# Splitting a gated chunk one chunk later in the feed-forward block of a decoder layer

## The chip, the cores and the metric

The kernel runs on one core of a Trainium2 chip. The metric is the device time of one execution in microseconds, as a median over runs. The profile is one more execution, with its own time; its clock starts at the first instruction of the span. The engines are named as in the profile: PE multiplies matrices and PEld loads their stationary operand, DVE and ACT do element work, POOL does a little of it, and SP issues nearly all DMA transfers in the order in which they stand in its queue.

## The reference

The reference is one decoder layer over 256 tokens of width 1024 in float32: a mixer of causal pooling and block attention, cross-attention into 256 memory tokens, and a dense gated feed-forward network of width 2816, each followed by a residual sum and a layer norm. The part that the change touches is the feed-forward network:

```python
def swiglu(h, w_gate, w_up, w_down):
    return (jax.nn.silu(h @ w_gate) * (h @ w_up)) @ w_down

        h = layer_norm(DEEPNORM_ALPHA * h + swiglu(h, w_gate[l], w_up[l], w_down[l]),
                       ln3_g[l], ln3_b[l])
```

## The kernel before

All large products are made of three matmuls. Each float32 operand is split into a high part, which is the operand rounded by a cast, and a low part, which is the operand minus its high part; the product is high by high, high by low and low by high (`three`, lines 256 to 258). A weight is loaded raw by a DMA from SP's queue (line 80), cast on ACT into its high part (line 99) and subtracted on DVE into its low part (line 100). The weights come as one long stream of pieces w0 to w124, each 128 partitions by 1024 numbers, 512 KB. Seven raw buffers and eight pairs of high and low buffers rotate: the cast of piece i writes the buffers of piece i - 8, and the load of piece i writes the raw buffer of piece i - 7. A piece is prepared (cast, subtracted, and further loads issued) while the matmuls of earlier pieces are being recorded, so casts, subtractions and loads stand in the engines' queues between other work, at the place where the program asked for them.

The feed-forward network works in 11 chunks of 256 columns of the hidden width, numbered 0 to 10. Chunk c uses pieces w(59+4c) to w(62+4c), which hold 256 columns of `w_gate` beside 256 of `w_up`. Per chunk there are eight steps of the inner dimension, each with three matmuls for either of two token tiles, so 48 matmuls with 512 output columns; the two results stand in two of four rotating PSUM banks, `pg`. Then, for either token tile, ACT takes the silu of the gate half (`gated`, line 784) and DVE multiplies it by the other half (line 785) into `sg`. This frees the bank. Four banks are two chunks' worth: PE may work on chunk c + 1 while chunk c waits for `gated`, and no further.

The product with `w_down` needs the gated values with the hidden dimension on the partitions, so each chunk is turned round through DRAM, in three recorded steps. `gated_out` transposes 32 by 32 blocks on DVE into `gs` (line 340) and writes them to DRAM as `gd` (line 343). `gated_in` reads them back as `gr` in four DMAs (line 350); these wait for the write. `gated_split` splits what came back into the high and low parts `gTh` (ACT, line 319) and `gTl` (DVE, line 320). `gs` and `gr` share three rotating buffers.

The order of each engine's queue is the order of the program text, which is written out by hand. The matmuls of a chunk are a generator; `run(gu, n)` records n more of its eight steps, and the three turning steps of the chunk before stand between them. `gated(c)` is recorded when the chunk's matmuls are.

After chunk 10 the generator `dn` records the product with `w_down`, pieces w103 to w124, one row of 128 hidden numbers each. Its first 16 rows go into four accumulators at once, which take the same four PSUM banks as `pg`: a row is six matmuls for token tile 0, into the banks that chunk 9 used, and then six for token tile 1, into the banks of chunk 10. Each half row is one step of `run(dn, n)`. The last six rows, w119 to w124, are done accumulator by accumulator, with the last layer norm behind each. Rows 2c and 2c + 1 use the values of chunk c.

Of the kernel before, what the change touches and what calls it, by code (L numbers as in the profile page):

```python
# [24 lines left out]
NFC = DFF // CW  # L25
# [16 lines left out]
class Stream:  # L42
# [61 lines left out]
    def get(self, numbers, k):  # L104

        n = self.src[numbers[0]].shape[1]
        self.prepare(numbers[k // n] + 1)
        self.asked += 1
        if not self.held and self.asked % self.pace == 0:
            self.prepare(min(self.used + AHEAD, len(self.tiles) + 1))  # L110
        hi, lo = self.tiles[numbers[k // n]]
        return hi[:, k % n, :], lo[:, k % n, :]
# [13 lines left out]
def decoder_layer(  # L126
# [18 lines left out]
    def bank(name):  # L145
        return pb.tile([P, 512], F32, tag="b", name=name)

    def accbank(name):
        return pa.tile([P, 512], F32, tag="acc", name=name)
# [130 lines left out]
    def proj_n(pss, numbers, yT, last=True):  # L280

        for k in range(KD):
            for t, ps in pss.items():
                three(ps, pair(yT, ALL, k, slice(t * P, (t + 1) * P)), ws.get(numbers, k), k == 0, k == KD - 1)
            if last:
                ws.done(numbers, k)
            yield

    def proj_rows(acc, chunks, get, pieces, first, last, free, again=False):

        last_k = sum(ws.rows(numbers) for numbers in chunks) - 1
        k0 = 0
        for numbers in chunks:
            nk = ws.rows(numbers)
            for t in sorted({piece[0] for piece in pieces}):
                for j in range(nk):
                    k = k0 + j
                    y = pair(get(k), ALL, slice(t * P, (t + 1) * P))
                    hi, lo = ws.get(numbers, j)
                    for piece in pieces:  # L300
                        if piece[0] == t:
                            s = slice(*piece[1:])
                            three(acc[piece], y, (hi[:, s], lo[:, s]), first and k == 0, last and k == last_k,
                                  again)
                    if free and t == pieces[-1][0]:
                        ws.done(numbers, j)
                    yield
            k0 += nk

    def run(gen, n=None):  # L310

        while n is None or n > 0:
            if next(gen, gen) is gen:
                return False
            n = None if n is None else n - 1
        return True

    def split(h, l, ps):
        nc.scalar.copy(h, ps)  # L319
        nc.vector.tensor_sub(l, ps, r32(h))  # L320
# [14 lines left out]
    def turned(blocks, n, name):  # L335

        st = sp.tile([P, 4, n, 32], F32, name=f"{name}s", tag="pair", bufs=3)
        for at, src in blocks:
            m = src.shape[1]
            nc.vector.transpose(st[:, :, at:at + m, :].rearrange("p j m b -> p m j b"),  # L340
                                src.rearrange("p m (j b) -> p m j b", b=32))
        via = hp.tile([P, 4, n * 32], F32, name=f"{name}d", tag="hop")
        nc.sync.dma_start(via, st.rearrange("p j m b -> p j (m b)"))
        return via

    def landed(via, n, name):

        raw = sp.tile([P, 4, n, 32], F32, name=f"{name}r", tag="pair", bufs=3)
        for j in range(4):
            nc.sync.dma_start(raw[32 * j:32 * (j + 1)].rearrange("p i m b -> p i (m b)"),  # L350
                              via[:, j, :].rearrange("(i a) r -> a i r", i=4))
        return raw
# [235 lines left out]
    class Norm:  # L588
# [11 lines left out]
        def sum(self, c0, c1, acc):  # L600
            s = slice(c0, c1)
            nc.vector.scalar_tensor_tensor(self.r[:, s], self.tok[:, s], ALPHA, acc, op0=OP.mult, op1=OP.add)  # L602
# [34 lines left out]
    def project(chunks, get, held, pieces=PIECES):  # L637

        acc = {piece: accbank("acc") for piece in PIECES}
        if pieces != PIECES:
            (*_, (_, _, c), _), last = pieces, PIECES[-1]
            acc[pieces[-2]], acc[pieces[-1]] = acc[last][:, :c - last[1]], bank("acc")[:, :last[2] - c]
        head, rest = chunks[:-held], chunks[-held:]
        done = sum(ws.rows(numbers) for numbers in head)
        if head:
            yield from proj_rows(acc, head, get, PIECES, True, pieces != PIECES, True)
        ws.prepare(ws.used + AHEAD)
        ws.prepare(ws.used + W_BUFS, nc.gpsimd)  # L650
        ws.held = True
        for piece in pieces:
            yield from proj_rows(acc, rest, lambda k: get(done + k), [piece], not head or piece[1] % 512 != 0, True,
                                 piece == pieces[-1], bool(head) and pieces != PIECES)
            yield piece, acc[last] if pieces != PIECES and piece == pieces[-2] else acc[piece]
# [125 lines left out]
    def gated(c, t, ps):  # L781

        sg = sgs[c][:, :, t, :]
        nc.scalar.activation(sg, ps[:, :CW].rearrange("p (f b) -> p f b", f=2), AF.Silu, bias=0.0, scale=1.0)  # L784
        nc.vector.tensor_mul(sg, sg, ps[:, CW:].rearrange("p (f b) -> p f b", f=2))  # L785
# [3 lines left out]
    def gated_out(c):  # L789
        via[c] = turned([(0, sgs[c].rearrange("p f t b -> p (f t) b"))], 4, "g")  # L790

    def gated_in(c):
        via[c] = landed(via[c], 4, "g")

    def gated_split(c):
        i, f = divmod(2 * c, KD)
        h, l = [g[:, f:f + 2, :].rearrange("p f (t i b) -> p (f t) i b", t=T, i=4) for g in gT[i]]
        split(h, l, via[c].rearrange("p i m b -> p m i b"))
# [12 lines left out]
    for c in range(1, NFC):  # L811
        sgs.append(sp.tile([P, 2, T, P], F32, name="sg", tag="pr", bufs=PR_BUFS))
        pss = {t: accbank("pg") for t in range(T)}
        gu = proj_n(pss, c_gu[c], h2T)
        run(gu, 1)
        gated_out(c - 1)
        run(gu, 2)
        gated_in(c - 1)
        run(gu, 4)
        gated_split(c - 1)  # L820
        run(gu)
        for t in range(T):
            gated(c, t, pss[t])
# [4 lines left out]

    pieces = PIECES[:3] + ((1, 512, 768), (1, 768, D))
    dn = project(c_dn, lambda k: (gT[k // KD][0][:, k % KD], gT[k // KD][1][:, k % KD]), 6, pieces)  # L830
    run(dn, 4)
    gated_out(NFC - 1)
    run(dn, 8)
    gated_in(NFC - 1)
    run(dn, 12)
    gated_split(NFC - 1)
    def finish(norm, t, at=None):

# [82 lines left out]
```

## Time and profile before

| | |
|---|---|
| median of 3 runs | 397.5 us (397.42 to 398.53) |
| the profiled execution's own time | 396.49 us |
| its span, first to last instruction | 394.7 us |
| mean granted TensorE clock | 0.978 |
| PE busy, share of the span | 374.2 us, 95% |
| DVE busy | 253.2 us, 64% |
| ACT busy | 175.2 us, 44% |
| DMA moved | 77.69 MB, mean 197 GB/s |

The rows of the profile's page name an engine, a line of the kernel, the tile written and the tile read, and how often. "Idle before it" is the time in which the engine stood still just before such an instruction, and the arrow names what came last of those things that it had to wait for. A row of a timeline gives the start in the span, the duration, and the same names. Matmuls are pipelined: the row of one lasts 0.39 us, but the next starts 0.23 us after it, so the starts are what counts.

### The profile page before, as it was taken

Reading aid. Unit: us, or ns where it says so; the run is one execution under the profiler, and the core shown is the slowest. Engines: PE = TensorE matmul, PEld = TensorE weight load, DVE = VectorE, ACT = ScalarE, POOL = GpSimd, SP = SyncE. Lnnn points to the kernel's source line nnn. Section 1 sums busy time; section 2 is a strip of 40 time slices with the busy share of each in tenths; the row PEclk is TensorE's granted clock in tenths of the full one; section 3 lists DMA queues with packets and bytes.
Section 4 is the critical chain, followed back from the end, with each engine's and each line's share of the span. In section 5 each row is a group of like instructions: output and inputs, shape, how many; then the busy total and the mean of one; then the engine's idle time right before and its main releaser. Section 6 shows DMA issues by size and latency. Waiting matters only on the chain.

```text
span 394.7 us, 5499 instructions
## 1 busy us (share of the span) xinstructions
PE 374.2 (95%) x2076; PEld 323.2 (82%) x2076; DVE 253.2 (64%) x371; ACT 175.2 (44%) x263; POOL 19.4 (5%) x31
## 2 busy tenths in 40 slices
PE   9999999999999999999999999999999719999991
PEld 9997989998888999988788888888787607888881
DVE  5768889754897765756895654556665355435175
ACT  5656677544244645543183553333555233344000
POOL 1000038000010000001000000000000000000000
PEclk9999999999999999999999999999999957999998
DMA  8996766658239644232058666765778765640011
GB/s 253 413 413 228 249 232 200 208 183 289 83 112 387 259 149 160 81 134 108 0 161 346 226 215 225 263 216 203 248 229 269 277 217 182 215 132 0 2 50 57
DMA packets 29386, 77.69 MB, mean 197 GB/s; under 512 B 3376, under 2 KB 10160, under 8 KB 29232
## 3 DMA queue, kind: packets, MB, share of 16 engines
q1 hardware_dynamic: 28784, 76.95, 55.6%
q10 hardware_dynamic: 576, 0.39, 0.3%
q8 instruction: 16, 0.26, 0.3%
q14 instruction: 10, 0.08, 0.1%
HBM read 73.40 MB, written 3.93 MB: 196 GB/s over the span
## 4 chain that ended last, share of the span: by engine, by line
PE 64%; DMA 16%; DVE 7%; ACT 5%; SPq 3%; issue 3%; ACTq 0%; DVEq 0%
DMA gd<-gs 11%; PE acc L256 9%; PE acc L257 9%; PE acc L258 9%; PE pqk L391 6%; PE pxq L274 6%; PE pxk L274 6%; DMA gr<-gd 5%; PE pu L274 3%; SPq L350 3%; PE xv L258 2%; PE xv L256 2%; PE xv L257 2%; DVE gs L340 2%; ACT sg L784 1%
## 5 line engine op out<-in xcount | busy, mean ns | idle before, releaser
L320 DVE TENSOR_TENSOR gTl<-gr,gTh 128x512 fp32r<-128x512 f32 x11 | 7.6, 692 | 50.9 <-ACT gTh L319 50.9
L319 ACT CAST gTh<-gr 128x512 fp32r<-128x512 f32 x11 | 6.8, 620 | 67.4 <-DMA gr<-gd 67.4
L613 POOL TENSOR_TENSOR rs<-rs,mhalf 128x1 f32<-128x1 f32 x6 | 5.4, 893 | 313.8 <-DVE rs L612 313.8
L256 PE MATMUL acc<-w103h,gTh 128*128 128x512 f32 x4 | 2.3, 578 | 11.2 <-DVE sg L785 11.2
L602 DVE SCALAR_TENSOR_TENSOR r<-h,acc 128x256 f32<-128x256 f32 (+1 forms) x10 | 5.1, 520 | 10.9 <-PE acc L258 10.9
L256 PEld LDWEIGHTS acc<-w103h,gTh 128*128 128x128 f32 x4 | 1.0, 248 | 12.5 <-DVE sg L785 12.4
L428 ACT ACTIVATE pr<-pr,mx 128x128 f32<-128x128 f32 (+1 forms) x16 | 7.1, 445 | 6.8 <-DVE mx L459 6.8
L605 DVE BATCH_NORM_STATS2 st<-r 128x6 f32<-128x512 f32 (+1 forms) x14 | 8.1, 580 | 0.5
L319 ACT CAST h2Th<-tp 128x512 fp32r<-128x512 f32 x4 | 2.3, 587 | 13.5 <-PE tp L330 13.4
L785 DVE TENSOR_TENSOR sg<-sg,pg 128x256 f32<-128x256 f32 x22 | 8.3, 414 | 0.0
L428 ACT ACTIVATE xpr<-xs,mx 128x256 f32<-128x256 f32 x8 | 3.7, 468 | 10.2 <-DVE mx L439 10.2
L618 DVE SCALAR_TENSOR_TENSOR r<-r,mv,g 128x512 f32<-128x512 f32 x11 | 7.8, 745 | 0.0
L340 DVE STREAM_TRANSPOSE gs<-sg 128x512 f32<-128x512 f32 x11 | 7.7, 704 | 0.0
L784 ACT ACTIVATE sg<-pg 128x256 f32<-128x256 f32 x22 | 7.3, 377 | 0.1
L503 POOL TENSOR_TENSOR win<-win 128x269 f32<-128x269 f32 (+2 forms) x6 | 6.5, 1082 | 0.5
L503 POOL TENSOR_TENSOR win<-upad 128x271 f32<-128x271 f32 x4 | 3.5, 872 | 54.3 <-ACT upad L531 54.3
L433 DVE RECIPROCAL sm<-sm 128x2 f32<-128x2 f32 x12 | 2.0, 167 | 5.9 <-ACT xpr L428 4.5
L624 DVE SCALAR_TENSOR_TENSOR h<-r,rs,b 128x512 f32<-128x512 f32 x8 | 5.6, 747 | 0.0
L319 ACT CAST h1Th<-tp 128x512 fp32r<-128x512 f32 x4 | 2.3, 587 | 7.1 <-PE tp L330 7.1
L330 PEld LDWEIGHTS tp<-ident,h 128*128 128x128 f32 x32 | 3.9, 141 | 1.6 <-issue 0.7
L330 PE MATMUL tp<-ident,h 128*128 128x128 f32 x32 | 4.8, 273 | 0.3 <-DVE h L624 0.3
L362 PE MATMUL busy<-const-float32-0.0 128*128 128x128 f32 x18 | 4.2, 428 | 0.8 <-PEq L885 0.8
(1091 smaller groups left out, 1422.8 us busy)
## 6 DMA issues: line engine op xcount, KB each, us to landing
gd<-gs SPq DMA_DIRECT2D x11, 256.0 KB, 3.7
gr<-gd SPq DMA_DIRECT2D x44, 64.0 KB, 2.1
g<-in_ln_g SPq DMA_DIRECT2D x3, 512.0 KB, 5.1
b<-in_ln_b SPq DMA_DIRECT2D x3, 512.0 KB, 7.5
wr<-in_w_qkv SPq DMA_DIRECT2D x5, 256.0 KB, 4.7
mr<-in_mem_t SPq DMA_DIRECT2D x1, 1024.0 KB, 11.7
xt<-in_x SPq DMA_DIRECT2D x1, 1024.0 KB, 8.3
xr<-in_x_t SPq DMA_DIRECT2D x3, 256.0 KB, 6.3
```

Source lines behind the costliest of these rows:

```text
L256: nc.tensor.matmul(ps, wa, ya, start=start, stop=False, skip_group_check=part)
L257: nc.tensor.matmul(ps, wa, yb, start=False, stop=False, skip_group_check=part)
L258: nc.tensor.matmul(ps, wb, ya, start=False, stop=stop, skip_group_check=part)
L274: nc.tensor.matmul(pss[f], w[:, s], y, start=k == 0 and f == 0 and n == 0, stop=k == KD - 1 and n == 2, skip_group_check=True)
L319: nc.scalar.copy(h, ps)
L330: nc.tensor.transpose(ps[:, k * P:(k + 1) * P], tok[:, (k0 + k) * P:(k0 + k + 1) * P], ident)
L340: nc.vector.transpose(st[:, :, at:at + m, :].rearrange("p j m b -> p m j b"), src.rearrange("p m (j b) -> p m j b", b=32))
L350: nc.sync.dma_start(raw[32 * j:32 * (j + 1)].rearrange("p i m b -> p i (m b)"), via[:, j, :].rearrange("(i a) r -> a i r", i=4))
L391: nc.tensor.matmul(qk[i][:, f, :], w[:, c * P:(c + 1) * P], y, start=k == 0 and f == 0 and w is hi and y is x_hi, stop=k == KD - 1 and w i ...
L428: nc.scalar.activation(dst[:, j, :], src[:, j, :], AF.Exp, bias=mx[:, j:j + 1], scale=sign, accum_out=sm[:, j:j + 1])
L503: nc.gpsimd.tensor_add(nxt[:, 2 * n - 1:], cur[:, 2 * n - 1:], cur[:, n - 1:PADW + S - n])
L784: nc.scalar.activation(sg, ps[:, :CW].rearrange("p (f b) -> p f b", f=2), AF.Silu, bias=0.0, scale=1.0)
```

## The change

The step `gated_split` moves from chunk c + 1, where it stood behind the seventh of eight matmul steps, to chunk c + 2, behind the third. The step `gated_in` stays in chunk c + 1 and moves from behind the third matmul step to behind the fifth. Behind the last chunk, in the product with `w_down`, the splits of chunks 9 and 10 both have to follow; the three steps of chunk 10 move forward there. No instruction is added or removed.

```diff
@@ -815,9 +815,10 @@
         run(gu, 1)
         gated_out(c - 1)
         run(gu, 2)
+        if c > 1:
+            gated_split(c - 2)
+        run(gu, 2)
         gated_in(c - 1)
-        run(gu, 4)
-        gated_split(c - 1)
         run(gu)
         for t in range(T):
             gated(c, t, pss[t])
@@ -828,11 +829,13 @@
 
     pieces = PIECES[:3] + ((1, 512, 768), (1, 768, D))
     dn = project(c_dn, lambda k: (gT[k // KD][0][:, k % KD], gT[k // KD][1][:, k % KD]), 6, pieces)
+    run(dn, 2)
+    gated_out(NFC - 1)
+    run(dn, 2)
+    gated_split(NFC - 2)
     run(dn, 4)
-    gated_out(NFC - 1)
-    run(dn, 8)
     gated_in(NFC - 1)
-    run(dn, 12)
+    run(dn, 10)
     gated_split(NFC - 1)
```

In ACT's queue, at the end of the last chunks, `gTh` is the high part of a chunk read back, `sg` the silu of a chunk's two token tiles, and `w106h` and the like are casts of weights:

```order
 L784 ACTIVATE sg<-pg 128x2x128 x2
 L99 CAST w106h<-w106r 128x1024
 L99 CAST w107h<-w107r 128x1024
+L319 CAST gTh_2047<-gr 128x512
 L99 CAST w108h<-w108r 128x1024
 L99 CAST w109h<-w109r 128x1024
-L319 CAST gTh_2047<-gr 128x512
 L784 ACTIVATE sg<-pg 128x2x128 x2
 L99 CAST w110h<-w110r 128x1024
 L99 CAST w111h<-w111r 128x1024
+L319 CAST gTh_2047<-gr 128x512
```

Here the first silu pair is chunk 9's and the second chunk 10's. The split that stood directly ahead of chunk 10's silu, that of chunk 9, now stands behind it and behind two casts; between the two silu pairs there is now the split of chunk 8, between the second and the third cast. DVE's queue is changed in the same way, with the subtractions and the multiplications of `sg` in place of casts and silus.

In SP's queue, in a chunk of the middle, with the write of a turned chunk (line 343), its four reads (line 350) and loads of weights (line 80):

```order
 L343 DMA gd<-gs 128x512
 L80 DMA w82r<-in_w_gu 128x1024
+L80 DMA w83r<-in_w_gu 128x1024
 L350 DMA gr<-gd 32x4x128 x4
-L80 DMA w83r<-in_w_gu 128x1024
 L80 DMA w84r<-in_w_gu 128x1024
```

The four reads now stand behind one more load of weights than before.

## The prediction

> **What bounds the kernel now.** I read the page first, to see which engine is the limit, then the list of waits.
>
> ```profile
> PE 374.2 (95%) x2076; PEld 323.2 (82%) x2076; DVE 253.2 (64%) x371; ACT 175.2 (44%) x263; POOL 19.4 (5%) x31
> L256 PE MATMUL acc<-w103h,gTh 128*128 128x512 f32 x4 | 2.3, 578 | 11.2 <-DVE sg L785 11.2
> ```
>
> ```profile
> PE acc L256 <- DVE sg L785: 11.2, 2, 9.1
> PE pg L256 <- DVE sg L785: 0.2, 1, 0.2
> ACT gTh L319 <- DMA gr<-gd: 67.4, 10, 8.3
> ```
>
> PE works 95% of the span, so most of what happens on other engines costs nothing. But PE has one large wait, 11.2 us in two pieces, at w103, the first row of the product with `w_down`. What it waits for there is DVE's multiplication of `sg`, which frees a PSUM bank. So the question is why a chunk's `sg` is late. The third wait row is the suspect: ACT stands 67.4 us in ten waits, before casting `gTh`, for data read back from DRAM. PE's timeline shows what this costs.
>
> ```profile
> 213.84 0.39 PE L256 MATMUL pg<-w67h,h2Th 128*128 128x512 f32 x1
> ...
> 301.06 0.39 PE L258 MATMUL pg<-w98h,h2Tl 128*128 128x512 f32 x1
> 301.65 0.50 PE L256 MATMUL pg<-w99h,h2Th 128*128 128x512 f32 x1 [0.20 <-DVE sg L785]
> ...
> 309.03 0.39 PE L258 MATMUL pg<-w101h,h2Tl 128*128 128x512 f32 x1
> ...
> 312.43 0.39 PE L258 MATMUL pg<-w102h,h2Tl 128*128 128x512 f32 x1
> 314.89 0.50 PE L256 MATMUL acc<-w103h,gTh 128*128 128x512 f32 x1 [2.08 <-DVE sg L785]
> ...
> 315.93 0.59 PE L257 MATMUL acc<-w103l,gTh 128*128 128x512 f32 x1
> 316.31 0.63 PE L258 MATMUL acc<-w103h,gTl 128*128 128x512 f32 x1
> 326.08 0.79 PE L256 MATMUL acc<-w103h,gTh 128*128 128x512 f32 x1 [9.14 <-DVE sg L785]
> ...
> 329.64 0.40 PE L258 MATMUL acc<-w104h,gTl 128*128 128x512 f32 x1
> ...
> 331.97 0.39 PE L256 MATMUL acc<-w105h,gTh 128*128 128x512 f32 x1
> ```
>
> The undisturbed step from matmul to matmul is (312.43 - 309.03) / 15 = 0.227 us, so a chunk of 48 takes 10.88 us. Chunk 2 begins at 213.84 (w67), chunk 10 at 301.65 (w99) and ends at 312.43 + 0.23 = 312.66. ACT's rows for the same stretch:
>
> ```profile
> 211.32 1.06 ACT L99 CAST w73h<-w73r 128x1024 fp32r<-128x1024 f32 x1 [1.25 <-PE pg L258]
> 219.72 0.62 ACT L319 CAST gTh<-gr 128x512 fp32r<-128x512 f32 x1 [7.34 <-DMA gr<-gd]
> 220.25 0.65 ACT L784 ACTIVATE sg<-pg 128x256 f32<-128x256 f32 x2
> ...
> 300.44 0.66 ACT L784 ACTIVATE sg<-pg 128x256 f32<-128x256 f32 x2
> ...
> 313.69 0.65 ACT L784 ACTIVATE sg<-pg 128x256 f32<-128x256 f32 x2
> ...
> 317.06 1.05 ACT L99 CAST w109h<-w109r 128x1024 fp32r<-128x1024 f32 x1
> 324.35 0.62 ACT L319 CAST gTh<-gr 128x512 fp32r<-128x512 f32 x1 [6.24 <-DMA gr<-gd]
> 324.87 0.65 ACT L784 ACTIVATE sg<-pg 128x256 f32<-128x256 f32 x2
> ```
>
> ACT takes its queue in order, and each split stands directly ahead of the next chunk's silu. So the silu of chunk 1, whose matmuls were done when chunk 2 began, runs 220.25 - 213.84 = 6.4 us late, and that of chunk 10 runs 324.87 - 312.66 = 12.2 us late. The silus follow a ring: silu, transposition, write to DRAM, read, split, next silu. Its last two rounds took 313.69 - 300.44 = 13.25 us and 324.87 - 313.69 = 11.18 us, both longer than PE's 10.88. The chain of waits shows which part made the longer one long, the write:
>
> ```profile
> 303.93 5.76 DMA gd<-gs
> ...
> 317.18 3.75 DMA gd<-gs
> ```
>
> The lag grows, and PE, which can be one chunk of 10.88 us ahead, first feels it at 301.65 and pays all of it when it turns to w103: 2.08 us for chunk 9's banks and 9.14 us for chunk 10's. The stage view adds the clock.
>
> ```profile
> 285.00:296.00 11.00, 11.00 (x50) 8.94 (x49) 6.58 (x8) 4.96 (x7) 0.00 (x0) 1.00 0.73 230
> 296.00:307.00 11.00, 10.80 (x49) 8.60 (x48) 6.30 (x8) 4.96 (x7) 0.00 (x0) 1.00 0.83 283
> ...
> 316.00:318.00 2.00, 0.94 (x3) 0.22 (x1) 2.00 (x3) 2.00 (x3) 0.00 (x0) 0.50 0.23 72
> ...
> 326.00:328.00 2.00, 1.92 (x5) 1.54 (x6) 1.58 (x3) 0.46 (x1) 0.00 (x0) 0.50 0.42 170
> 332.00:343.00 11.00, 11.00 (x50) 9.13 (x49) 4.90 (x4) 4.22 (x4) 0.00 (x0) 1.00 0.66 216
> ```
>
> The third number from the end is the granted clock: 1.00 before, 0.50 after the gaps, 1.00 again from 332. So a slow start belongs to the price of the wait.
>
> **The change part by part.** *The stall removed.* From the last matmul of chunk 10 (312.43) to the first of w105 (331.97) are 25 steps. Undisturbed they take 25 x 0.227 = 5.67 us; they took 19.54. The difference, 13.87 us, holds both waits and the slow clock (19.54 - 5.67 - 2.08 - 9.14 = 2.65 us for clock and restarts). At 301.06 to 301.65 a step took 0.59 instead of 0.23: another 0.36. Together 14.2 us, if the silus come in time.
>
> *Do they?* With the split out of the way, what stands ahead of a silu on ACT is a cast. The cast ahead of chunk 10's silu is w109, which overwrites w101's buffers and so waits for PE, as w73's did at 211.32. PE is done with w101 one piece (12 x 0.227 = 2.72 us) before the chunk's end, at about 309.9; the cast takes 1.05 and ends near 311.2, and DVE's subtraction 1.2 us later, near 312.4. Both engines are then free when the matmuls end at 312.43 + 0.39 = 312.82. DVE's rows give the rest:
>
> ```profile
> 314.43 0.74 DVE L785 TENSOR_TENSOR sg<-sg,pg 128x256 f32<-128x256 f32 x2
> 315.31 1.23 DVE L100 TENSOR_TENSOR w106l<-w106r,w106h 128x1024 fp32r<-128x1024 f32 x1
> 316.45 0.70 DVE L340 STREAM_TRANSPOSE gs<-sg 128x512 f32<-128x512 f32 x1
> ```
>
> From the silu's start at 313.69 to PE's restart at 314.89 were 1.20 us, so the first of chunk 10's banks is free by 312.82 + 1.20 = 314.02, the second half a multiplication pair (0.37) later. PE's first half row of w103 uses chunk 9's banks, free long before, and lasts six steps, from 312.66 to 314.02. So the new wait is bounded by nothing below and by one more cast ahead of the silu (1.05 us) above; I take nothing, since the banks come free just as PE asks.
>
> *The reads moved.* Let T be the start of a chunk on PE. The silu pair starts at about T + 0.2, and by the rows above the transposition ends 317.15 - 313.69 = 3.5 us later, at T + 3.7; the write lands 3.75 to 5.76 us after that, at T + 7.5 to T + 9.5. The reads now stand behind two loads of weights whose raw buffers come free with the second and the third subtraction of the chunk. These wait for casts, and those for PE: the third cast for two pieces of 2.72 us, T + 5.4, its subtraction ends at T + 7.8. So the reads are issued between T + 8.2 and T + 9.6. What they take:
>
> ```profile
> 320.94 1.75 SPq L350 DMA_DIRECT2D gr<-gd  x4
> 322.79 0.38 SPq L80 DMA_DIRECT2D w115r<-in_w_down  x1
> ```
>
> ```profile
> DMA to landing us min/median/max: 1.9/2.1/3.4
> ```
>
> Four issues take 1.75 us and the last lands 1.9 to 3.4 us behind: between T + 11.8 and T + 14.7, thus 0.9 to 3.8 us into the next chunk. There the split stands behind a cast that waits for the chunk's first piece, and is due at 2.72 + 0.2 + 0.95 = 3.9 us. It hardly waits. If it is late, two casts (0.95 each) follow before the next silu at 11.1, so it may start as late as 8.6 us into the chunk without delaying anything: at least 4.8 us to spare. The Trainium skill, "DMA: Bandwidth & Descriptors", section "Queues, rings and completion order", says that an engine takes the descriptors of one queue in ring order, so that reads behind a fresh weight load would pay for that load first; the 3.4 us at the top of the row above may hold such a case, and the margin covers another.
>
> *The loads moved.* One weight load now passes ahead of the reads, which is earlier for it. All loads now follow PE's pace, and the largest landing times are:
>
> ```profile
> w111r<-in_w_down SPq DMA_DIRECT2D x1, 512.0 KB, 3.3
> ...
> b<-in_ln_b SPq DMA_DIRECT2D x1, 512.0 KB, 8.0
> ```
>
> A raw buffer is refilled when the piece seven earlier is subtracted, and its own cast comes seven pieces of 2.72 us later, 19 us, less 2.2 us for that cast and subtraction: 17 us against 8.0 at most. If this cover were gone, every us of lateness beyond it would stop PE. A chunk moves four loads of 512 KB, a write and a read of 256 KB, 2.62 MB in 10.88 us, 241 GB/s; the rows above show 283 GB/s at a DMA share of 0.83.
>
> *Behind chunk 10.* The split of chunk 9 stands behind w111's cast and that of chunk 10 behind w118's, which waits for w110, the eighth row: 8 x 2.72 = 22 us into the product. Its reads stand behind loads that wait for the fourth of these rows and are issued about 11 us in. The last six rows, which alone need them, begin after 16 x 2.72 = 43.5 us. Nothing is owed there: 0.
>
> *Sum.* 14.2 us off, nothing on. The profiled execution would go from 396.49 (394.7 span and 1.8 around it) to 382.3, with a span of 380.5. The median of the runs lies 1.0 above that execution, so I predict 397.5 - 14.2 = **383.3 us**.
>
> **The rivals.** *A small wait stays* at w103: the last silu stands behind a late cast or split and PE meets a gap like the 2.08 us at 314.89, with the clock lowered behind it. The rows at 315.93 and 316.31 last 0.59 and 0.63 instead of 0.39, after that gap alone. From 326.08 to 329.64 eight steps took 3.56 us instead of 1.81, so a slow start costs about 1.8 us. That gives 383.3 + 2.1 + 1.8 = 387.2. For it: the cast of w109 ends only 1.6 us before the matmuls do. Against it: that is still time enough. By the Trainium skill, "TensorE: Matmul & The Clock Gate", section "Why this matters for your kernels", the clock stays up over idle gaps below about 3 us, and this rival would cost only its 2.1 us, 385.4. By that rule the clock should not have dropped at 315.93; the trace disagrees.
>
> *The split still holds up the silu*: the reads land over 8.6 us into the next chunk, and the lag is as now, 397.5 us. It needs reads 4.8 us later than my late bound; no row comes near.
>
> *Slower: a new ring through SP.* A split stands ahead of two casts, the third subtraction of the chunk releases the load ahead of the next reads, and the next split waits for them. Its round is split 0.62, cast 0.95, subtraction 1.2, load issue 0.4, reads 1.75 and landing 1.9 to 3.4: 6.8 to 8.3 us, below PE's 10.88. If its round were longer, the silus, which stand behind those casts, would lag by the excess in each of nine rounds, and it decides against the change from 10.88 + 12.2 / 9 = 12.2 us on. At the longest round of the present ring, 13.25, the lag would be 9 x 2.37 = 21.3 us in place of 12.2, so 397.5 + 9.1 = 406.6. It would need another 5 us in a round, from reads that queue behind several loads.
>
> **How the numbers follow.** Forecast 0.80, small wait 0.13, split still ahead 0.04, new ring 0.03. Both first cases are faster; 0.3%, 1.2 us, is about what these runs can tell from no change, and the third case counts as that. So faster 0.93, same 0.04, slower 0.03. The range runs from 382.0, the sum with a tenth of a us or so gained at further steps and the scatter of a us seen in the runs, to 387.2, where the small wait stays.
>
> **What would show it.** Right: no wait of PE for `sg` at w103 over 0.5 us, the clock at 1.00 from 200 to the end of PE's work, silus within 0.5 us of a chunk's last matmul, and casts of weights on ACT that wait for PE in every chunk, w75 on. ACT's 67 us of waiting for `gr` should shrink to a few us, most of it at the first splits. Wrong: silus that still start later than their chunk's end by a growing lag, reads landing over 8.6 us into the next chunk, or a wait of PE for a weight piece.

## The result

| | before | after |
|---|---|---|
| median | 397.46 us | 381.01 us |
| lowest to highest | 397.34 to 398.53 | 380.87 to 381.55 |
| profiled execution, its span | 396.49, 394.7 | 381.07, 379.3 |
| mean granted TensorE clock | 0.978 | 0.997 |

The ratio is 0.9583, with a 95% interval of 0.9564 to 0.9602: 16.4 us less. The prediction was 383.3 us with a range from 382.0 to 387.2, so direction and mechanism came out, but the time lies 1 us below the range.

The page of the kernel after, its row of PE and the shares of the chain that ended last:

```profile
PE 370.6 (98%) x2076; PEld 322.2 (85%) x2076; DVE 256.7 (68%) x371; ACT 179.4 (47%) x263; POOL 19.3 (5%) x31
...
PE 96%; DVE 2%; issue 0%; ACT 0%; DVEq 0%
```

Before, DMA held 16% of that chain. Now PE's own work is nearly all of it. The list of waits of the kernel after has only two for PE, and neither is for `sg`: one stands at the start of the program, the other, of 0.3 us, in chunk 0. ACT waits for PE ahead of its silus, and hardly for reads:

```profile
ACT sg L784 <- PE pg L258: 12.8, 20, 1.0
...
ACT gTh L319 <- DMA gr<-gd: 3.0, 2, 2.9
...
PE busy L362 <- PEq L888: 0.8, 1, 0.8
PE tp L330 <- DVE h L624: 0.3, 1, 0.3
```

PE's timeline where chunk 10 ends and the product with `w_down` begins, and the row at which token tile 1 first needs chunk 10's banks:

```profile
311.29 0.39 PE L258 MATMUL pg<-w102h,h2Tl 128*128 128x512 f32 x1
311.52 0.39 PE L256 MATMUL acc<-w103h,gTh 128*128 128x512 f32 x1
...
312.88 0.39 PE L256 MATMUL acc<-w103h,gTh 128*128 128x512 f32 x1
...
316.96 0.39 PE L256 MATMUL acc<-w105h,gTh 128*128 128x512 f32 x1
```

The 25 steps from 311.29 to 316.96 take 5.67 us, where they took 19.54. ACT's and DVE's rows at that place:

```profile
309.00 1.05 ACT L99 CAST w109h<-w109r 128x1024 fp32r<-128x1024 f32 x1 [1.67 <-PE pg L258]
311.04 0.38 ACT L784 ACTIVATE sg<-pg 128x256 f32<-128x256 f32 x1 [0.98 <-PE pg L258]
311.72 0.39 ACT L784 ACTIVATE sg<-pg 128x256 f32<-128x256 f32 x1 [0.29 <-PE pg L258]
...
315.40 0.61 ACT L319 CAST gTh<-gr 128x512 fp32r<-128x512 f32 x1
```

```profile
311.45 0.42 DVE L785 TENSOR_TENSOR sg<-sg,pg 128x256 f32<-128x256 f32 x1
312.13 0.42 DVE L785 TENSOR_TENSOR sg<-sg,pg 128x256 f32<-128x256 f32 x1 [0.26 <-ACT sg L784]
```

The silu pair no longer runs in one go. Its first half starts at 311.04, ahead of the chunk's last matmul, as soon as token tile 0 is complete; the first bank is free at 311.87, 1.0 us before PE asks for it at 312.88. The split of chunk 9 (315.40) finds its data there: no wait stands at its row. The reads themselves became slower:

```profile
308.62 0.33 SPq L80 DMA_DIRECT2D w115r<-in_w_down  x1
309.04 1.80 SPq L350 DMA_DIRECT2D gr<-gd  x4
```

```profile
DMA to landing us min/median/max: 2.7/4.4/5.4
```

They are issued 0.4 us behind a load of 512 KB and land 4.4 us after issue in the median, where it was 2.1. With a chunk more of time nobody notices.

### The profile page after: what moved, and what is told of

Its sections match the earlier page's. It is cut to its first block, busy times and chain, and to the rows that moved or that the text cites. A ratio compares the mean times of both kernels' runs of the same rounds, so it can differ in the third digit from the quotient of the medians.

```text
span 379.3 us, 5500 instructions
## 1 busy us (share of the span) xinstructions
PE 370.6 (98%) x2076; PEld 322.2 (85%) x2076; DVE 256.7 (68%) x371; ACT 179.4 (47%) x263; POOL 19.3 (5%) x31
## 4 chain that ended last, share of the span: by engine, by line
PE 96%; DVE 2%; issue 0%; ACT 0%; DVEq 0%
PE pg L258 10%; PE pg L256 10%; PE pg L257 10%; PE acc L256 9%; PE acc L258 9%; PE acc L257 9%; PE pqk L391 6%; PE pxq L274 6%; PE pxk L274 6%; PE pu L274 3%; PE xv L258 2%; PE xv L257 2%; PE xv L256 2%; PE busy L362 1%; PE pv L256 1%; PE tp L330 1%
## 5 line engine op out<-in xcount | busy, mean ns | idle before, releaser
L784 ACT ACTIVATE sg<-pg 128x256 f32<-128x256 f32 x22 | 8.4, 384 | 12.9 <-PE pg L258 12.8
L785 DVE TENSOR_TENSOR sg<-sg,pg 128x256 f32<-128x256 f32 x22 | 9.3, 421 | 3.9 <-ACT sg L784 2.7
L324 DVE SCALAR_TENSOR_TENSOR xq<-pxq,xq 128x512 fp32r<-128x512 f32 x4 | 2.8, 691 | 3.3 <-ACT xq L323 3.3
L323 ACT ACTIVATE xq<-pxq 128x512 fp32r<-128x512 f32 x4 | 2.4, 597 | 5.3 <-PE pxq L274 5.3
```

## The experiments

The theory: in the kernel before a ring sets the pace, from silu over transposition, write, reads and split to the next silu, and its round is longer than PE's 10.88 us per chunk. The rivals are named in the texts on record. On the chips of these experiments the kernel before took 398.7 to 399.6 us, 1 to 2 us more than on the first; comparisons are with it on the same chip.

### The parts of the change, one at a time

Only the split moved, with the part behind chunk 10 as in the kernel after (part of the loop, against the kernel after):

```diff
         if c > 1:
             gated_split(c - 2)
-        run(gu, 2)
         gated_in(c - 1)
         run(gu)
```

> Only the split is moved, one chunk later; the read stays behind the third matmul step. Theory (the split no longer stands ahead of the silu, and that is the gain): 381.0 us within 0.5, no wait of PE at w103; the reads land 2 us after issue as before, not 4.4. Rival (the later read matters, it gets out of the way of weight loads): a time clearly above 381, at least a third of the 16.4 us given back, 386 or more.

Measured: 381.25 us, ratio 0.9546 (0.9518 to 0.9574), no wait of PE for `sg`, reads landing 2.0 us after issue in the median. The split alone brings the whole gain.

Only the read moved (against the kernel before):

```diff
-        run(gu, 2)
+        run(gu, 4)
         gated_in(c - 1)
-        run(gu, 4)
+        run(gu, 2)
         gated_split(c - 1)
```

> Only the read is moved, behind the fifth step; the split stays directly ahead of the silu. Theory (a ring of silu, transposition, write, read, split sets the pace): the reads stand behind one more weight load, and in the kernel after such reads land 4.4 us after issue instead of 2.1. Each round is longer by what this adds, 0.5 to 2.3 us in ten rounds: 402 to 420 us, and PE's waits for sg grow by the same. Rival (the read's place is free or helps): 397.5 or less.

Measured: 413.15 us, ratio 1.0348 (1.0313 to 1.0384), 14 us slower than before. Its waits, and the landing of its reads:

```profile
PE acc L256 <- DVE sg L785: 11.5, 1, 11.5
PE pg L256 <- DVE sg L785: 11.0, 5, 3.0
```

```profile
DMA to landing us min/median/max: 2.1/3.8/6.7
```

PE now waits for `sg` inside the block too. The silus of its profile run from 221.17 (chunk 1) to 341.36 (chunk 10): nine rounds of 13.35 us. The kernel before, on the same chip, has 219.69 to 327.09: 11.93 us. So the half of the change that looks harmless costs 1.4 us in every round as long as the ring exists: the reads queue behind one more load, and land 3.8 us after issue in the median instead of the 2.2 of the kernel before on this chip.

Only the part behind chunk 10 (against the kernel before):

```diff
-    run(dn, 4)
+    run(dn, 2)
     gated_out(NFC - 1)
-    run(dn, 8)
+    run(dn, 6)
     gated_in(NFC - 1)
-    run(dn, 12)
+    run(dn, 10)
     gated_split(NFC - 1)
```

> The loop over the chunks is as before; only the last chunk's write, read and split are issued earlier in the product with w_down, as in the kernel after. Theory: the wait at w103 is made by silus recorded ahead of this part, so 397.5 us within 1 us and the same 11 us of waits. Rival (part of the gain comes from the new order behind chunk 10): up to 14 us less, 383 to 395.

Measured: 399.54 us, ratio 0.9993 (0.9971 to 1.0015). This part brings nothing.

### Is it the place or the distance?

One chunk later, but at the old place, directly ahead of the silu (against the kernel after):

```diff
-        run(gu, 2)
-        if c > 1:
-            gated_split(c - 2)
-        run(gu, 2)
+        run(gu, 4)
         gated_in(c - 1)
+        run(gu, 2)
+        if c > 1:
+            gated_split(c - 2)
         run(gu)
```

> The split is issued one chunk later, but at the old place, behind the seventh step and directly ahead of the silu; the read behind the fifth step. Theory (the wait counts, not the place): the data has landed some 8 us before, ACT has about 1 us free ahead of each silu and the split takes 0.62, so 381 to 382 us and no wait at w103. Rival (the split's own work ahead of the silu is what delays it): 0.6 us more per round and a wait at w103 of several us, 385 or more.

Measured: 381.88 us, ratio 0.9553 (0.9512 to 0.9593), no wait of PE for `sg`. The place ahead of the silu costs nothing once the data is there.

The other way round, in the same chunk as before, but behind that chunk's silu (against the kernel before):

```diff
         gated_in(c - 1)
-        run(gu, 4)
-        gated_split(c - 1)
         run(gu)
         for t in range(T):
             gated(c, t, pss[t])
+        gated_split(c - 1)
```

> The split stays in the same chunk as before, but stands behind that chunk's silu instead of ahead of it; read and write as before. Theory (what costs is that a silu stands behind a wait for DRAM): the silus come within 1 us of the chunk's last matmul, PE does not wait at w103, 381 to 382 us, though the reads land only as the chunk ends and ACT waits for them up to 1 us per chunk. Rival (a whole chunk of delay is needed, since ACT still waits for the reads ahead of the next casts): 385 us or more.

Measured: 389.35 us, ratio 0.9748 (0.9701 to 0.9795). This went against the theory as I had put it: only some 10 us are gained, and PE still waits 5.9 us at w103. ACT's rows:

```profile
254.35 0.62 ACT L319 CAST gTh<-gr 128x512 fp32r<-128x512 f32 x1 [6.43 <-DMA gr<-gd]
254.88 1.05 ACT L99 CAST w86h<-w86r 128x1024 fp32r<-128x1024 f32 x1
...
258.68 0.64 ACT L784 ACTIVATE sg<-pg 128x256 f32<-128x256 f32 x2
265.39 0.62 ACT L319 CAST gTh<-gr 128x512 fp32r<-128x512 f32 x1 [6.08 <-DMA gr<-gd]
```

From split to split are 265.39 - 254.35 = 11.04 us, again more than 10.88, though no silu lies in between on the way. The ring closes without it: behind the split stands the cast of w86, behind that on DVE its subtraction and the next transposition, then write and reads. The silu (258.68) comes late because it stands behind four casts that stand behind the split. So the ring is not made by the silu. It is made by any wait for the reads that stands ahead of the next chunk's transposition, with only one chunk between them.

### The round against 10.88 us

Transposition and write directly behind the multiplication (against the kernel before), first with the reads where they were, then with the reads behind the first step:

```diff
-        run(gu, 1)
         gated_out(c - 1)
-        run(gu, 2)
+        run(gu, 3)
         gated_in(c - 1)
```

> The order before, with one thing moved: the transposition and the write stand directly behind the multiplication, ahead of the next chunk's first matmul step, so one cast and subtraction leave the ring. Theory (the round of the ring against PE's 10.88 us decides): a round shrinks by 1.28 us (transposition 2.76 us behind the silu's start before, 1.48 now) to 9.9 to 10.4; the lag of 6.4 us after chunk 1 shrinks instead of growing, and is 0 to 3 us at chunk 10: 381 to 386 us. Rival (any split that waits for DRAM ahead of the silu costs, whatever the round): 393 or more.

Measured: 399.79 us, ratio 0.9988 (0.9955 to 1.002): nothing gained, a miss of the expectation. SP's rows and the landing of the reads show where it went:

```profile
244.66 0.33 SPq L343 DMA_DIRECT2D gd<-gs  x1
245.77 0.33 SPq L80 DMA_DIRECT2D w89r<-in_w_gu  x1
246.91 0.33 SPq L80 DMA_DIRECT2D w90r<-in_w_gu  x1
247.35 1.96 SPq L350 DMA_DIRECT2D gr<-gd  x4
```

```profile
DMA to landing us min/median/max: 2.6/4.9/6.4
```

The write is issued earlier and no longer right behind a load, and it is done within the 2.7 us until the reads go. But with the write two loads instead of one pass ahead of the reads, the second 0.4 us ahead. The reads land 4.9 us after issue instead of 2.2. What the engines' order gave, the DMA queue took back.

```diff
-        run(gu, 1)
         gated_out(c - 1)
-        run(gu, 2)
+        run(gu, 1)
         gated_in(c - 1)
-        run(gu, 4)
+        run(gu, 6)
         gated_split(c - 1)
```

> As the kernel with the early transposition (which moved write and transposition ahead of the chunk's first step, and left 399.8 us unchanged), but the reads stand behind the first step, so that one weight load lies between write and reads instead of two. The split is where it was before, directly ahead of the silu. Theory (the ring of silu, transposition, write, read, split against PE's 10.88 us, with every weight load queued ahead of write or reads in it): the reads land 2 to 2.5 us after issue instead of 4.9, a round is 9.5 to 10.6 us, the lag of 6 us after chunk 1 shrinks to 0 to 3 us at chunk 10, and the time is 381 to 386 us without the change. Rival (a split in the chunk directly before cannot be in time, whatever the order): 395 or more.

Measured: 382.33 us, ratio 0.956 (0.9528 to 0.9592). Of its four executions the profiled one took 1529 us, and the other three 381.81 to 382.57; so the kernel ran again for a trace:

> The kernel with transposition and write moved ahead of the chunk's first step and the reads behind it, again, for a trace to read (the profiled execution of the run before was disturbed and cannot be read). Theory: 381.8 to 382.6 us; rounds of the ring below 10.88 us, so that the silus catch up from a lag of 6 us at chunk 1 to less than 1 us at chunk 10; reads landing 2 to 3 us after issue; PE without a wait at w103. Rival (the time is reached in another way, with the silus still late by a chunk): a lag of 5 us or more at chunk 10 that PE somehow does not meet.

Measured: 382.10 us, ratio 0.9566 (0.9522 to 0.961), no wait of PE for `sg`. The silus of chunks 1 to 5 in ACT's rows:

```profile
218.55 0.65 ACT L784 ACTIVATE sg<-pg 128x256 f32<-128x256 f32 x2
...
228.62 0.65 ACT L784 ACTIVATE sg<-pg 128x256 f32<-128x256 f32 x2
...
237.92 0.65 ACT L784 ACTIVATE sg<-pg 128x256 f32<-128x256 f32 x2
...
247.69 0.65 ACT L784 ACTIVATE sg<-pg 128x256 f32<-128x256 f32 x2
...
257.42 0.89 ACT L784 ACTIVATE sg<-pg 128x256 f32<-128x256 f32 x2
```

Rounds of 10.07, 9.30, 9.77 and 9.73 us: now shorter than 10.88, and the lag of 4.3 us after chunk 1 (chunk 2 begins at 214.21 here) is gone by chunk 5. It is not gone for good: chunk 9's silu comes at 303.32, 2.1 us behind the chunk's end at 301.25, and chunk 10's is in time again. The split still waits for its reads in the old place, and it costs nothing:

```profile
ACT gTh L319 <- DMA gr<-gd: 18.8, 7, 5.3
```

This is the same gain as the change's, by order alone and without the extra chunk of distance. It does not beat the kernel after (381.60 beside it, below).

The ring made longer, transposition and write one weight piece later, in the kernel before and in the kernel after:

```diff
-        run(gu, 1)
+        run(gu, 3)
         gated_out(c - 1)
         run(gu, 2)
         gated_in(c - 1)
-        run(gu, 4)
+        run(gu, 2)
         gated_split(c - 1)
```

> The order before with the transposition and the write one weight piece later (behind the third step, the read behind the fifth), so a further subtraction of 1.1 us lies in each round; one weight load lies between write and read, as before. Theory (ring): ten rounds of 1.1 us more, so 11 us over the kernel before, 408 to 411 us, with PE waiting for sg in most of the last chunks. Rival (the lag is not made by the ring but by the startup and the last loads): within 3 us of the kernel before.

Measured: 419.58 us, ratio 1.0505 (1.0448 to 1.0562). 20 us more, twice what I expected. SP's rows:

```profile
253.81 0.35 SPq L80 DMA_DIRECT2D w89r<-in_w_gu  x1
254.95 0.33 SPq L80 DMA_DIRECT2D w90r<-in_w_gu  x1
255.57 0.33 SPq L343 DMA_DIRECT2D gd<-gs  x1
256.68 0.33 SPq L80 DMA_DIRECT2D w91r<-in_w_gu  x1
260.68 2.00 SPq L350 DMA_DIRECT2D gr<-gd  x4
```

The write follows two loads directly and takes 260.68 - 255.57 = 5.1 us until the reads may go. Over the chunks this is 5.3 us in the median, against 4.0 in the kernel before on that chip. With the 1.1 us of the subtraction this about makes up the difference of the rounds: the silus of this profile run from 221.94 to 350.20, nine rounds of 14.25 us, 2.3 more than 11.93. The same move where the split comes a chunk later:

```diff
-        run(gu, 1)
+        run(gu, 3)
         gated_out(c - 1)
-        run(gu, 2)
         if c > 1:
             gated_split(c - 2)
```

> The kernel after, with transposition and write one weight piece later, as in the kernel with the long ring, where this cost 20 us. Theory (one chunk later the way through DRAM has two chunks, 21.8 us, and spends 13 to 14): nothing is lost, 381 to 382 us and no wait of PE. Rival (the wait is only pushed back and each us of the way still counts): 384 or more.

Measured: 381.69 us, ratio 0.9552 (0.9525 to 0.9579), no wait of PE for `sg`. What costs 20 us in the one arrangement costs nothing in the other.

### What a gap of PE costs

Idle copies on ACT ahead of chunk 10's silu, seven and eleven of them; nothing is left out of the computation:

```diff
+        if c == NFC - 1:
+            pad = sp.tile([P, 512], F32, name="pad", tag="pad", bufs=1)
+            for _ in range(7):
+                nc.scalar.copy(pad, h2[:, 0, 0:512])
         for t in range(T):
             gated(c, t, pss[t])
```

> The kernel after, with seven idle copies on ACT (128x512, 0.53 us apart) ahead of chunk 10's silu: its banks come free at about 314.9 in the span instead of 312.6, and PE, which asks at 312.88, stands still for 2.0 us once. By the trace of the kernel before (after its gap of 2.08 us the matmuls at 315.93 and 316.31 were slow) the clock drops and another 1.8 us goes: 381.0 + 3.8 = 384.8. Rival (Trainium skill, TensorE: Matmul & The Clock Gate, Why this matters for your kernels: gaps below about 3 us leave the clock up): 383.0 and a granted clock of 1.00 throughout.

> The same with eleven idle copies: a gap of 4.1 us. By either view the clock drops to about half for some 3.5 us behind it: 381.0 + 4.1 + 1.8 = 386.9, against 385.1 if it does not.

Measured: 383.86 us (383.39 to 385.85), ratio 0.9617, with seven, and 389.55 us, ratio 0.9736, with eleven. PE's row behind the gap and the stage behind it, for seven:

```profile
315.38 0.50 PE L256 MATMUL acc<-w103h,gTh 128*128 128x512 f32 x1 [2.24 <-DVE sg L785]
```

```profile
315.00:317.00 2.00, 1.62 (x7) 1.36 (x8) 1.54 (x3) 1.08 (x2) 0.00 (x0) 1.00 0.04 14
```

and for eleven:

```profile
318.71 0.80 PE L256 MATMUL acc<-w103h,gTh 128*128 128x512 f32 x1 [4.84 <-DVE sg L785]
```

```profile
319.00:321.00 2.00, 2.00 (x5) 1.54 (x5) 1.56 (x2) 0.41 (x1) 0.00 (x0) 0.50 0.00 0
```

After 2.24 us the clock stayed at 1.00 and the gap cost 2.3 us over the 381.6 us of the kernel after. After 4.84 us it stood at 0.50, the 18 steps from 318.71 took 6.75 us instead of 4.08, and the whole came to 8.0 us. The rule of the Trainium skill ("TensorE: Matmul & The Clock Gate", section "Why this matters for your kernels") that gaps below about 3 us leave the clock up agrees with both. Other traces of this case do not agree with it. Two gaps of the kernel with the long ring:

```profile
279.63 0.50 PE L256 MATMUL pg<-w87h,h2Th 128*128 128x512 f32 x1 [2.29 <-DVE sg L785]
...
281.25 0.63 PE L256 MATMUL pg<-w87h,h2Th 128*128 128x512 f32 x1
...
294.34 0.58 PE L256 MATMUL pg<-w91h,h2Th 128*128 128x512 f32 x1 [1.89 <-DVE sg L785]
294.72 0.63 PE L257 MATMUL pg<-w91l,h2Th 128*128 128x512 f32 x1
```

Behind the gap of 2.29 us the matmuls turn slow (0.63 us instead of 0.39) after 1.3 us, behind that of 1.89 us at once. In the kernel with only the read moved the same slowness follows gaps of 2.27 and 2.11 us, with a granted clock of 0.50 from 250.2 to 253.4, but not those of 2.04 and 1.62. So the reading of the trace of before, that a gap of 2.08 us can bring the slow clock, holds, and the run with seven copies is one of those where it did not come. In the traces of these runs no gap up to 1.62 us brought it in the feed-forward block or the product with `w_down`, and every one from 3.0 us on did; what decides in between is not shown. Behind the four gaps of 1.89 to 2.29 us the 18 steps took 5.8 to 5.9 us, so a slow start cost 1.7 to 1.8 us there, as I had counted; behind 4.84 us it cost 2.7.

### What scatters

The kernel before, again:

> The kernel before, once more, to see how much it scatters. My sum added the 1.0 us by which the median of the kernel before lay above its profiled execution to the kernel after as well; there profile and median agree (381.07 and 381.01). Theory: the 1 us is scatter of the ring through DRAM, so it sits in PE's wait at w103: executions of this kernel differ by about 1 us in span, and in a new profile the waits at w103 differ from 11.2 us by about as much as the spans differ from 394.7, with all other parts equal to 0.3 us. Rival: the whole span scatters, at the start and the end too; then the last matmul of chunk 1 (213.6) and the stretch from the last matmul to the end (8.2 us) differ by as much.

Measured: 399.07 us (398.37 to 401.20), ratio 0.9993. Its profile, with a span of 397.2 instead of 394.7:

```profile
PE acc L256 <- DVE sg L785: 11.8, 2, 9.6
PE pg L256 <- DVE sg L785: 1.9, 4, 0.8
```

```profile
213.63 0.39 PE L256 MATMUL pg<-w67h,h2Th 128*128 128x512 f32 x1
...
388.99 0.28 PE L258 MATMUL acc<-w124h,gTl 128*128 128x256 f32 x1
```

Chunk 2 begins at 213.63 (213.84 in the first profile), and from the last matmul to the end are 8.2 us in both. The difference of 2.5 us lies in between, and 2.3 of it are waits for `sg`: 13.7 us against 11.4. Between these two profiles, the scatter sits in the ring.

The kernel after, beside the kernel before on such a chip:

> The kernel after, beside the kernel before on the chip of the experiments, where the kernel before took 399.3 to 399.6 us instead of 397.5. Theory (what scatters and differs from chip to chip is the ring through DRAM, which sets the time before and not after): the kernel after takes 380.9 to 381.8 us here too, so the gain is 17.5 to 18.5 us, and executions lie within 1 us. Rival (the chip is slower as a whole by 0.5%): 382.7 to 383.5, the gain stays 16.4.

Measured: 381.60 us (381.23 to 381.80) against 398.73 (397.86 to 401.34), ratio 0.9556 (0.9520 to 0.9592). The gain is 17.1 us there, between the two expectations, but the time is the theory's. The kernel after took 0.6 us more than on the first chip; its first matmul for `v` came at 28.55 instead of 27.81, so this is its start. Its executions lie within 0.6 us of each other, those of the kernel before within 3.5.

## Why the prediction was right and where it missed

**The wait and its cause** were right. The ring, the lag of the silus and the two waits at w103 were as read, with one refinement: the silu need not be part of the ring, as the run with the split behind it showed. The waits, the slow clock behind them and the restarts went: 14.0 us from the first matmul of chunk 10 to that of w105 (30.32 us before, 16.32 after), where the sum had 13.87.

**The silus in time:** right, with more room than I gave. I let the first silu start with the chunk's last matmul and found the bank free just as PE asks; its half only needs token tile 0, and there is 1.0 us to spare.

**The reads moved:** issue at 309.04 is 8.4 us into chunk 10, inside the 8.2 to 9.6 forecast. The landing was under-sized: 4.4 us in the median and 5.4 at most, against a bound of 3.4 taken from the rows of before. The Trainium skill's rule on ring order ("DMA: Bandwidth & Descriptors", section "Queues, rings and completion order"), which I let the margin cover, agrees with the rows. The margin did cover it: only the splits of chunks 0 and 3 waited, 2.87 and 0.17 us, and PE never for `sg`.

**The loads and the part behind chunk 10** owed nothing, as said: no wait of PE for a weight, and 399.54 us for the part behind chunk 10 alone.

**The sum is the step that failed,** in two terms of about equal size. It had 14.2 us off; from profile to profile it was 15.4. Of these 1.2 us, 0.41 in all were lost at the starts of chunks 8 and 9, which the trace of before shows and which I put at nothing (I took only the 0.36 at chunk 10), and another 0.1 at the first steps of chunk 10; 0.24 us at the start and 0.38 at the end are differences of these two executions outside the changed part. The other term is "the median of the runs lies 1.0 above that execution", added to the kernel after. In the kernel after, median and profile agree within 0.1 us. So that 1.0 us went with the change too: the kernel before scatters, its profiled execution was a short one, and by the two profiles above its scatter sits in the ring, which the kernel after no longer has on its path. 15.4 + 1.0 is the 16.4 measured. The range's lower end had the same fault: it allowed a us downward for scatter, from a middle 2.3 us too high.

**The rivals:** no small wait stayed, the split did not hold up the silu, and no new ring formed, not even with the split late ahead of the silu or with the longer way through DRAM. With the landings of 4.4 to 5.4 us, the new ring's round would be 9.3 to 10.3 us by the prediction's own terms instead of 6.8 to 8.3, an estimate: still below 10.88, with less to spare than I gave. The first rival's claim, that a gap of 2 us can bring a slow start of 1.8 us, failed in the one run made to test it and held in the kernels with only the read moved and with the long ring.

## What to carry to other kernels

A round trip through DRAM that ends in an in-order engine's queue makes a ring with whatever stands behind it and leads to the next round trip; compare its round with the time of one step of the loop, and either shorten it below that or give it two steps. Count the loads that stand ahead of its write and its reads in the DMA queue as part of the round: moving a transfer behind one more load cost 1.4 us per round here, and moving an engine's instruction earlier gained nothing until the transfers' order followed. When a change takes a scattering wait off the path, expect the median to fall by that wait's median, not by what it is in one profile.

## What the runs showed of the hardware

Reads of 64 KB issued 0.4 us behind a load of 512 KB in the same queue land 4.4 us after issue in the median (kernel after), against 2.1 us where the last load went some 2.5 us ahead of them (kernel before); I had bounded this by 3.4. And the length of a gap of PE does not decide alone, near 2 us, whether the clock stays up. Gaps of 2.24 (seven copies) and 2.04 us (only the read moved) left it at 1.00, while gaps of 2.08 (kernel before), 2.11 and 2.27 (only the read moved), 1.89 and 2.29 us (long ring) were followed within 1.3 us by matmuls at half speed. What else decides is open.
